# Two transformer blocks on one core: the order of seven block products, and where their neighbours' tiles lie

## The chip, the core and the metric

The kernel runs on one core of a Trainium2 chip, in one launch. The metric is the device time in microseconds (us), as the median of several runs. TensorE (PE) multiplies, ScalarE (ACT) and VectorE (DVE) move results out of its accumulation banks and prepare its operands, GpSimd (POOL) and SyncE (SP) issue most of the transfers. All engines run side by side, each through its own queue in order.

## What is computed

1,024 tokens of width 1,024 go through two blocks. The first is attention, a residual layer norm, and a feed-forward part with a short convolution; the second is a gated linear attention and a squared-ReLU feed-forward part. The two feed-forward parts are what the change is about:

```python
def conv_ffn(x, w_up, conv_w, conv_b, w_down):          # first block, d_ff 2816
    u = x @ w_up
    u = sum(u_pad[:, j:j + s, :] * conv_w[j] for j in range(3)) + conv_b
    value, gate = jnp.split(u, 2, axis=-1)
    return (value * jax.nn.gelu(gate)) @ w_down
def sqrelu_mlp(h, w1, w2):                              # second block, d_ff 4096
    return jnp.square(jax.nn.relu(h @ w1)) @ w2
x = layer_norm(DEEPNORM_ALPHA * x + mix, ln1_g, ln1_b)  # ahead of conv_ffn
h_lat = h_lat + mod_l[2] * o_lat                        # ahead of sqrelu_mlp
```

All is float32. The kernel makes each product of three passes: both operands are split into a high part (a rounded copy) and a low part (the rest), and high·high, high·low and low·high are summed.

## The kernel before

The stages run one after the other. Attention takes the first 500 us of the profile. `mixed` (L1006) then multiplies by `w_out`, normalizes and leads into the first **up pass** (609 to 1083 us); `ffn_down` (L1071) is the first **down pass**, with the context half of the second block woven in (1085 to 1405); the gated attention follows (to 1790); `o_projection` (L1267) multiplies by `w_o`, adds the residual and leads into the second up pass (1928 to 2279); `mlp_down` (L1314) is the second down pass and the end (from 2291).

**The up pass** (`up_pass`, L704) works on pairs of 128 weight columns, 22 pairs in the first block and 16 in the second. A pair is a 2x2 block product done with seven block multiplications in place of eight (Winograd's form). On the right stand seven fixed operands made from the activations, four in `hi`/`lo`, three in the extra tile `E` (`operands`, L675, writes them one token tile at a time). On the left stand A11, A12, A22 (the weights, loaded as `a` and `b`), and sums of them S1 to S4 (`sums`, L713). `parts` (L699) splits each into high and low; those tiles come from a ring of four slots (`ring`, L730), three of which a pair uses, and a smaller tile for S4. The loads and sums of a pair run more than one pair ahead of its products.

One `product` (L736) is twelve matmuls of 512 columns. The seven go into three accumulation banks X, Y and Z of eight. X is used for four partial sums in turn: after each product ACT copies X out, and the next product adds onto it, which it may do only when that copy has been read. The result is gathered in `ga` and `gb` in SBUF. The lines of the loop (L764 to L778), with their products in the order of the program:

```python
X  = A11·B11   -> ACT.copy(ga[xs], X)                       # L765, L766
Z  = A12·B21   -> DVE: ga[xs] = Z + ga[xs]                  # L767, L768
X += S2·T2     -> ACT.copy(ga[ys], X)                       # L769, L770
Y  = S1·T1                                                  # L771
X += S3·T3     -> ACT.copy(gb[ys], X)                       # L772, L773
                  DVE: gb[ys] = Y + gb[ys]                  # L774
Y += S4·B22    -> DVE: ga[ys] = Y + ga[ys]                  # L775, L776
X += A22·T4    -> ACT.copy(gb[xs], X)                       # L777, L778
```

TensorE keeps this order (`issue_after`, L739). The first pair is done in two halves of 256 columns, since the last token tiles come late. `finish` then runs on `ga` and `gb`: `conv_gate` (L1050) in the first block, with two ACT passes at L1055, four DVE passes at L1056 and L1057, a GELU, a product, and a store to HBM; `relu2` (L1301) in the second. In the first block `ga` and `gb` are the same two tiles for every pair; in the second they alternate.

**Ahead of the up pass** `square_product` (L622) makes each token tile in two halves of 512 columns, and `done` adds the residual, normalizes the row (a square with a sum on ACT, an inverse root on POOL), transposes (`rows`, L650) and calls `operands`. In `o_projection` the residual comes half a row at a time into the one buffer of pool `xp` (L1280, L1281). While the last tiles go through this, `up_pass` already loads and splits the first pair's A11, A12 and S2 (L719 to L722).

**The down pass** (`down_group`, L782) works on groups of hidden chunks (four in the second block). Each chunk is loaded back from HBM (`gload`, L789) and split, its weights likewise (`wdraw`, L795), and 16 units (8 token tiles by 2 halves) accumulate over the group and are added to `res`. Its pools (L1075, L1317) are laid on the bytes that the up pass has left, from the lowest address up, in the order in which they are opened; with `reuse_waits="tile"` a tile waits for the old tiles on its own bytes alone. Instructions are laid out by a scheduler that works through a modelled timeline when the kernel is built: what it puts first in an engine's queue comes first.

Of the kernel before, what the change touches and what calls it, by code (L numbers as in the profile page):

```python
# [17 lines left out]
P = 128  # L18
D = 1024
# [35 lines left out]
def build(tc, I, out, dbg=None, stop=None):  # L55
# [83 lines left out]
    convc = const.tile([P, 2 * NCH, 4], F32, name="convc")  # L139
# [48 lines left out]
    def attention_phase():  # L188
# [106 lines left out]
        for t, n in ((cs, "cs"), (convc, "conv"), (ng, "norms"), (adab, "ada_b_p"), (ghead, "ghead")):  # L295
            SP.dma_start(out=t, in_=I[n])
# [353 lines left out]
    def rows(src, t, scale=None, shift=None, by_row=None):  # L650

        if by_row is not None:
            diag = small.tile([P, P], F32, tag="diag", name="diag", bufs=2)
            DVE.tensor_scalar(out=diag, in0=ident, scalar1=by_row, scalar2=None, op0=ALU.mult)
# [20 lines left out]
    def operands(t, E, sp):  # L675
# [8 lines left out]
        split(by_k(u), E[0][:, 8:12, toks(t)], E[1][:, 8:12, toks(t)])  # L684
        DVE.tensor_tensor(out=b1[:, YS], in0=b1[:, YS], in1=u, op=ALU.subtract)
        DVE.tensor_tensor(out=b2[:, XS], in0=b2[:, YS], in1=b2[:, XS], op=ALU.subtract)
        split(by_k(b1), E[0][:, 0:8, toks(t)], E[1][:, 0:8, toks(t)])
        split(by_k(b2), hi[:, :, toks(t + 4)], lo[:, :, toks(t + 4)])

    def open_ext(st, n):  # L690
        pl = pool(st, n, 1, side="right")
        return [pl.tile([P, 12, 512], F32R, name=f"{n}_{x}") for x in ("hi", "lo")]

    def right_operands(E):

        at = {"B11": (0, 0, 0), "B21": (0, 4, 0), "T3": (0, 0, 512), "B22": (0, 4, 512), "T1": (1, 0, 0), "T4": (1, 4, 0), "T2": (1, 8, 0)}
        return {n: [tuple(a[:, k0 + k, c0:c0 + 512] for a in ((hi, lo), E)[e]) for k in range(4)] for n, (e, k0, c0) in at.items()}
# [6 lines left out]
    def up_pass(W, pairs, E, w0, room, finish):  # L704
# [16 lines left out]
        A1 = parts(a, w0)  # L721
        S20 = parts(ga[:, YS], w0, 512, "s")  # L722
# [7 lines left out]
        def ring():  # L730
            rot.rotate(-1)
            return rot[0]

        B = right_operands(E)
# [10 lines left out]
        for n in range(pairs):  # L745
            if n == 0:
                a, b, ga, gb = first
                A11, A12 = A1
                (S2,) = S20
                (S1,) = parts(ga[:, XS], w2, 512, "q")  # L750
                (S4,) = parts(gb[:, XS], w2, 512, "q")
                S3, A22 = parts(b, ring())
            else:
# [3 lines left out]
                A11, A12 = parts(a, ring())  # L757
                S1, S2 = parts(s, ring())
                (S4,) = parts(u, w2, 512, "q")
                S3, A22 = parts(b, ring())  # L760
# [696 lines left out]
```

## Time and profile before

| | |
|---|---|
| median of 3 runs | 2659.89 us (2654.38 to 2660.42) |
| the profiled execution | 2664.75 us, span 2663.0 us, mean granted TensorE clock 0.982 |
| TensorE, VectorE, ScalarE, GpSimd busy | 2498.9, 1640.1, 1154.2, 384.6 us |
| TensorE busy in the first, second up pass (609 to 1085, 1930 to 2279) | 435.4 of 476, 314.9 of 349 us |
| TensorE busy in the second down pass (2291 to 2606) | 312.5 of 315 us |

Busy time of TensorE counts each matmul to its modelled end, so matmuls overlap in it, and 100% is not the peak. The span leaves out 1.75 us of the profiled execution. Waits are named by what ended them.

### The profile page before, as it was taken

To read this page: it belongs to the slowest core of one execution; us is meant where nothing else is said; L and a number is where in the kernel's file an instruction comes from. 1 tells how busy PE (TensorE), PEld (TensorE's weight loads), DVE (VectorE), ACT (ScalarE), POOL (GpSimd) and SP (SyncE) were. 2 spreads that over 40 slices of the span, in tenths; PEclk is the share of its full clock that TensorE was granted. 3 is DMA by queue.
4 is the path that set the end of the run, shared out by engine and by line. 5 is a ranking of instruction groups with operands and counts; after the bars stand their busy time and mean duration, and the time that the engine had idled before them with its cause. 6 is when DMAs were issued, how large, how long until landed. Compare 5 with 4: busy or idle time off the path is not lost. (4 is left out here: it accounts for less than half of the span.)

```text
span 2663.0 us, 36063 instructions
## 1 busy us (share of the span) xinstructions
PE 2498.9 (94%) x13146; PEld 2117.1 (79%) x13146; DVE 1640.1 (62%) x3069; ACT 1154.2 (43%) x2046; POOL 384.6 (14%) x591
## 2 busy tenths in 40 slices
PE   8999999997999999899999999999879999899997
PEld 8898888776777777688888988997767777688885
DVE  5767675677776676587568666535754443355574
ACT  5555565544444444633236444323444444421212
POOL 4675623310000000000021000001100000000000
PEclk9999999998999999999999999999989999899998
DMA  5333322332222211645311211213322222543332
GB/s 169 109 87 103 91 73 83 120 124 95 74 77 79 79 72 48 208 148 184 110 72 59 74 52 60 74 36 128 107 95 96 102 95 86 173 144 101 121 107 91
DMA packets 130609, 266.81 MB, mean 100 GB/s; under 512 B 16376, under 2 KB 48760, under 8 KB 130432
## 3 DMA queue, kind: packets, MB, share of 16 engines
q1 hardware_dynamic: 120224, 227.81, 26.8%
q0 software_dynamic: 10208, 36.71, 3.4%
q8 instruction: 103, 1.69, 0.3%
q14 instruction: 74, 0.61, 0.1%
HBM read 205.17 MB, written 50.89 MB: 96 GB/s over the span
## 5 line engine op out<-in xcount | busy, mean ns | idle before, releaser
L130 PE MATMUL down<-wdh,gh 128*128 128x512 f32 x864 | 336.6, 397 | 24.1 <-ACT gh L102 12.3
L131 PE MATMUL down<-wdl,gh 128*128 128x512 f32 x864 | 338.3, 393 | 0.6 <-DVE wdl L103 0.6
L132 PE MATMUL down<-wdh,gl 128*128 128x512 f32 x864 | 333.8, 392 | 0.1
L130 PE MATMUL s<-act_hi,uh 128*128 128x512 f32 (+1 forms) x640 | 251.2, 393 | 67.9 <-DVE res L774 56.3
L132 PE MATMUL s<-act_hi,ul 128*128 128x512 f32 (+1 forms) x640 | 246.6, 385 | 3.0 <-DVE ul L103 3.0
L131 PE MATMUL s<-act_lo,uh 128*128 128x512 f32 (+1 forms) x640 | 246.4, 385 | 0.0
L130 PEld LDWEIGHTS down<-wdh,gh 128*128 128x128 f32 x864 | 163.6, 190 | 62.2 <-ACT gh L102 13.1
L130 PEld LDWEIGHTS s<-act_hi,uh 128*128 128x128 f32 x640 | 123.0, 192 | 107.4 <-DVE res L774 72.8
L569 POOL TENSOR_TENSOR rstd<-rstd,mhalf 128x1 f32<-128x1 f32 x74 | 55.2, 748 | 1012.3 <-DVE rstd L568 571.7
L131 PEld LDWEIGHTS down<-wdl,gh 128*128 128x128 f32 x864 | 164.0, 190 | 34.5 <-DVE wdl L103 1.3
L132 PEld LDWEIGHTS down<-wdh,gl 128*128 128x128 f32 x864 | 162.8, 189 | 35.2 <-DVE gl L103 1.1
L103 DVE TENSOR_TENSOR ul<-res,uh 128x1024 fp32r<-128x1024 f32 (+1 forms) x82 | 97.1, 1184 | 147.9 <-ACT uh L102 147.9
L130 PE MATMUL s<-ext_hi,uh 128*128 128x512 f32 (+1 forms) x480 | 183.2, 382 | 2.9 <-ACT res L766 2.9
L131 PE MATMUL s<-ext_lo,uh 128*128 128x512 f32 (+1 forms) x480 | 183.1, 382 | 0.0
L132 PE MATMUL s<-ext_hi,ul 128*128 128x512 f32 (+1 forms) x480 | 183.1, 381 | 0.0
L102 ACT CAST wdh<-wdraw 128x512 fp32r<-128x512 f32 x108 | 66.8, 622 | 194.0 <-PE down L132 71.0
L130 PE MATMUL tokp<-wh,act_hi 128*128 128x256 f32 (+1 forms) x512 | 147.3, 290 | 1.5 <-ACT wh L102 1.5
L132 PE MATMUL tokp<-wh,act_lo 128*128 128x256 f32 (+1 forms) x512 | 146.7, 288 | 1.9 <-DVE act_lo L103 1.9
L131 PE MATMUL tokp<-wl,act_hi 128*128 128x256 f32 (+1 forms) x512 | 147.5, 289 | 0.0
L132 PEld LDWEIGHTS s<-act_hi,ul 128*128 128x128 f32 x640 | 123.2, 192 | 27.1 <-DVE ul L103 3.3
L131 PEld LDWEIGHTS s<-act_lo,uh 128*128 128x128 f32 x640 | 123.3, 193 | 22.4
L369 ACT ACTIVATE P<-P,mx 128x640 f32<-128x640 f32 (+7 forms) x128 | 94.4, 738 | 77.6 <-DVE mx L366 73.6
(325 smaller groups left out, 6303.7 us busy)
## 6 DMA issues: line engine op xcount, KB each, us to landing
ada_w<-in_ada_w SPq DMA_DIRECT2D x192, 128.0 KB, 2.2
res<-in_w_up SPq DMA_DIRECT2D x44, 512.0 KB, 3.5
res<-in_mlp_w SPq DMA_DIRECT2D x32, 512.0 KB, 3.5
g2d<-res POOLq DMA_DIRECT2D x32, 512.0 KB, 2.9
wdraw<-in_mlp_w SPq DMA_DIRECT2D x64, 256.0 KB, 2.9
gload<-g2d SPq DMA_DIRECT2D x32, 512.0 KB, 3.5
g1d<-res POOLq DMA_DIRECT2D x22, 512.0 KB, 2.9
wdraw<-in_w_down SPq DMA_DIRECT2D x44, 256.0 KB, 3.3
```

What stands on the lines that cost most here:

```text
L102: ACT.copy(h, raw)
L103: DVE.tensor_tensor(out=l, in0=raw, in1=h, op=ALU.subtract)
L130: PE.matmul(out=o, lhsT=ah, rhs=bh, start=first, stop=False, **kw)
L131: PE.matmul(out=o, lhsT=ah, rhs=bl, start=False, stop=False, **kw)
L132: return PE.matmul(out=o, lhsT=al, rhs=bh, start=False, stop=last, **kw)
L369: ACT.activation(Pm[:, 0:W], Pm[:, 0:W], AF.Exp, bias=mx[:, 0:1], scale=-1.0, accum_out=mx[:, 1:2])
L569: POOL.tensor_tensor(out=t[:, 1:2], in0=t[:, 0:1], in1=mhalf, op=ALU.pow)
```

## The change

1. **Order of the products.** In `up_pass` Y = S1·T1 goes to second place and is copied at once into `gb[xs]` by ACT, S2·T2 follows, then Z. The addition that used to read Y at L774 now adds two SBUF tiles, after the product S4·B22. There is one ACT copy more in a pair, and the parts of `b` are split ahead of those of S4.
2. **First pair.** S1 and S2 are both split ahead of the pass, in pool `w0`; S3, A22 and S4 of the first pair get a high priority. The ring's four slots are laid anew.
3. **Down pools.** A function `down_pools` lays weights, raw loads, the rest and the chunk tiles in that order; the second down pass has eight weight slots for six, and groups of 2, six times 4, 3 and 3 chunks in place of eight times 4.
4. **Residual rows.** In `o_projection` the residual is loaded as whole rows straight into `res[t]`, after the last weight load of that batch, with no buffer between; pools there wait by tile.
5. **Small things.** The convolution weights are loaded at the start of the up pass, not at the start of the kernel; the squares of the row norms are written into `E` and not into a tile of their own; the diagonal tile of `rows` and `E` move to other pools or are cut in two tiles.

```diff
-    def up_pass(W, pairs, E, w0, room, finish):
+    def up_pass(W, pairs, E, w0, room, finish, setup=None):
...
         sums(a, b, ga, gb[:, XS])
-        A1 = parts(a, w0)
-        S20 = parts(ga[:, YS], w0, 512, "s")
+        A1, S12 = parts(a, w0), parts(ga, w0, tag="s")
         yield
...
-        w1, sw, w2 = (pool(st, n, b, reuse_waits="tile") for n, b in (("uw1", 1), ("usw", 2), ("uw2", 2)))
-        rot = deque((w0, w1, w2, w2))
+        sw, w2 = (pool(st, n, 2, reuse_waits="tile") for n in ("usw", "uw2"))
+        rot = deque(((w0, "s"), (w2, "w"), (w2, "w"), (w0, "w")))
...
-                (S2,) = S20
-                (S1,) = parts(ga[:, XS], w2, 512, "q")
-                (S4,) = parts(gb[:, XS], w2, 512, "q")
-                S3, A22 = parts(b, ring())
+                S1, S2 = S12
+                with tc.high_priority():
+                    S3, A22 = ring(b)
+                    (S4,) = parts(gb[:, XS], w2, 512, "q")
...
-                X, Z, Y = acc("s", m), acc("s", m), acc("s", m)
+                X, Y, Z = acc("s", m), acc("s", m), acc("s", m)
                 product(X, A11, "B11", True, cols)
                 ACT.copy(ga[:, xs], X)
+                product(Y, S1, "T1", True, cols)
+                ACT.copy(gb[:, xs], Y)
+                product(X, S2, "T2", False, cols)
+                ACT.copy(ga[:, ys], X)
                 product(Z, A12, "B21", True, cols)
                 DVE.tensor_tensor(out=ga[:, xs], in0=Z, in1=ga[:, xs], op=ALU.add)
-                product(X, S2, "T2", False, cols)
-                ACT.copy(ga[:, ys], X)
-                product(Y, S1, "T1", True, cols)
                 product(X, S3, "T3", False, cols)
                 ACT.copy(gb[:, ys], X)
-                DVE.tensor_tensor(out=gb[:, ys], in0=Y, in1=gb[:, ys], op=ALU.add)
                 product(Y, S4, "B22", False, cols)
                 DVE.tensor_tensor(out=ga[:, ys], in0=Y, in1=ga[:, ys], op=ALU.add)
+                DVE.tensor_tensor(out=gb[:, ys], in0=gb[:, xs], in1=gb[:, ys], op=ALU.add)
                 product(X, A22, "T4", False, cols)
                 ACT.copy(gb[:, xs], X)
...
+    def down_pools(st, n, w, mid, g):
...
+        wa = [pl(f"wd{i}", 2) for i in range(2)]
+        wdr, gr = pl("wdr", 2), pl("gr", 2)
+        wa.append(pl("wd2", w - 4))
...
+        mids = [pl(*m) for m in mid]
+        return (wdr, gr, in_turn("gp", g), wdp), mids
...
         def done(t, half, psum, last):
             c = slice(half * 512, half * 512 + 512)
             r = res[t]
-            x = xp.tile([P, 512], F32, tag="x", name="x2res")
-            SP.dma_start(out=x, in_=x2d[t][:, c])
-            DVE.tensor_tensor(out=r[:, c], in0=psum, in1=x, op=ALU.add)
+            if t not in seen:
+                with tc.issue_after(last.ins):
+                    SP.dma_start(out=r, in_=x2d[t])
+            DVE.tensor_tensor(out=r[:, c], in0=psum, in1=r[:, c], op=ALU.add)
...
-        groups = [list(range(i, i + 4)) for i in range(0, NMLP, 4)]
+        groups = [[0, 1]] + [list(range(i, i + 4)) for i in range(2, NMLP - 6, 4)] + [list(range(i, i + 3)) for i in (NMLP - 6, NMLP - 3)]
```

## Rows read from the trace of the kernel before

**Rows 1.** The page: busy time of TensorE, and the granted clock in 40 slices of the span.
```profile
PE 2498.9 (94%) x13146; PEld 2117.1 (79%) x13146; DVE 1640.1 (62%) x3069; ACT 1154.2 (43%) x2046; POOL 384.6 (14%) x591
...
PEclk9999999998999999999999999999989999899998
```

**Rows 2.** Groups of instructions over the whole span: line, engine, operation, tiles, count, then busy us, mean ns of one, and idle time of the engine ahead of them with what ended it.
```profile
L130 PE MATMUL s<-act_hi,uh 128*128 128x512 f32 (+1 forms) x640 | 251.2, 393 | 67.9 <-DVE res L774 56.3 <-ACT uh L102 6.7 <-ACT res L770 4.5
```

**Rows 3.** The chain that ended last, in order of time (start us, us, what), over one pair of the second up pass.
```profile
2000.03 0.59 ACT res L773
2000.65 0.70 DVE res L774
2001.39 0.51 PE s L130
...
2021.57 0.70 DVE res L774
```

**Rows 4.** Timeline of TensorE in the up passes: start us, duration us, the matmul, and in brackets the idle time ahead of it. First two matmuls without a wait, 56 steps apart, then the first and the last of the 36 waits of this kind.
```profile
1060.57 0.39 PE L131 MATMUL s<-ext_lo,uh 128*128 128x512 f32 x1
...
1073.39 0.39 PE L130 MATMUL s<-act_hi,uh 128*128 128x512 f32 x1
...
659.37 0.50 PE L130 MATMUL s<-act_hi,uh 128*128 128x512 f32 x1 [1.40 <-DVE res L774]
...
2273.39 0.51 PE L130 MATMUL s<-act_hi,uh 128*128 128x512 f32 x1 [1.40 <-DVE res L774]
```

**Rows 5.** Busy time by stretch: from:to, length, then busy us and count of PE, weight loads, DVE, ACT, POOL, then the granted clock, the share of the DMA engines and GB/s.
```profile
590.00:643.00 53.00, 38.33 (x232) 34.79 (x231) 42.33 (x66) 25.24 (x40) 5.76 (x8) 0.84 0.25 90
699.00:720.00 21.00, 19.60 (x86) 15.78 (x85) 14.75 (x17) 9.46 (x11) 0.53 (x1) 1.00 0.21 75
1083.00:1112.00 29.00, 21.21 (x89) 15.75 (x88) 22.69 (x31) 25.14 (x42) 3.27 (x4) 0.94 0.96 339
1910.00:1965.00 55.00, 35.83 (x231) 33.68 (x232) 37.01 (x66) 24.64 (x45) 4.29 (x7) 0.78 0.25 80
2000.00:2021.00 21.00, 19.53 (x84) 15.70 (x84) 8.85 (x11) 9.96 (x13) 1.06 (x2) 1.00 0.27 101
2279.00:2296.00 17.00, 5.45 (x14) 4.16 (x14) 4.44 (x8) 6.39 (x7) 1.06 (x2) 0.60 0.87 292
2560.00:2606.00 46.00, 43.47 (x192) 35.65 (x192) 35.20 (x54) 8.34 (x13) 0.00 (x0) 1.00 0.44 143
```

**Rows 6.** Timeline of VectorE in one pair of the first up pass.
```profile
953.70 0.69 DVE L714 TENSOR_TENSOR s<-res 128x512 f32<-128x512 f32 x1 [1.55 <-DMA res<-in_w_up]
...
956.24 0.68 DVE L776 TENSOR_TENSOR res<-s,res 128x512 f32<-128x512 f32 x1
...
959.44 1.22 DVE L103 TENSOR_TENSOR ul<-res,uh 128x1024 fp32r<-128x1024 f32 x1
960.57 1.28 DVE L1057 SCALAR_TENSOR_TENSOR res<-res,convc,res 128x1022 f32<-128x1022 f32 x1
```

**Rows 7.** Timeline of ScalarE in the same pair.
```profile
956.96 1.25 ACT L1055 ACTIVATE res<-res,convc 128x1024 f32<-128x1024 f32 x1 [1.29 <-DVE res L776]
...
961.94 0.59 ACT L766 COPY res<-s 128x512 f32<-128x512 f32 x1 [1.04 <-DVE res L1057]
...
968.78 1.05 ACT L102 CAST uh<-res 128x1024 fp32r<-128x1024 f32 x1 [1.93 <-PE s L131]
```

**Rows 8.** Timeline of TensorE in the first pair of each up pass: matmuls with a wait ahead of them.
```profile
622.70 0.39 PE L130 MATMUL s<-act_hi,uh 128*128 128x256 f32 x1 [4.54 <-ACT res L770]
...
1939.99 0.58 PE L130 MATMUL s<-act_hi,uh 128*128 128x256 f32 x1 [6.75 <-ACT uh L102]
...
1948.52 0.58 PE L130 MATMUL s<-act_hi,uh 128*128 128x256 f32 x1 [2.24 <-DVE res L774]
```

**Rows 9.** Timeline of VectorE at the end of `o_projection`: the last two additions of the residual.
```profile
1915.27 0.69 DVE L1282 TENSOR_TENSOR res<-sq,x2res 128x512 f32<-128x512 f32 x1 [1.62 <-DMA x2res<-x2d]
...
1919.20 0.69 DVE L1282 TENSOR_TENSOR res<-sq,x2res 128x512 f32<-128x512 f32 x1 [1.71 <-DMA x2res<-x2d]
```

**Rows 10.** Timeline of TensorE at the start of the two down passes and of the last group: matmuls with a wait.
```profile
1085.62 0.95 PE L130 MATMUL down<-wdh,gh 128*128 128x512 f32 x3 [2.14 <-ACT wdh L102]
...
1095.74 0.50 PE L130 MATMUL down<-wdh,gh 128*128 128x512 f32 x1 [3.15 <-ACT res L1088]
...
2290.74 0.80 PE L130 MATMUL down<-wdh,gh 128*128 128x512 f32 x1 [11.55 <-ACT gh L102]
...
2605.13 0.74 PE L130 MATMUL down<-wdh,gh 128*128 128x512 f32 x2 [2.53 <-ACT wdh L102]
```

**Rows 11.** Timeline of SyncE's queue at the end of the second up pass.
```profile
2279.62 0.42 SPq L618 DMA_DIRECT2D fg<-in_final_g  x1
2280.09 0.95 SPq L789 DMA_DIRECT2D gload<-g2d  x2
```

**Rows 12.** The view of the `res` tiles in the first up pass: time from a DMA's issue to its landing, of the weight loads.
```profile
DMA to landing us min/median/max: 2.9/3.4/4.4
```

**Rows 13.** The same line in the view of the tile `gload`: all loads of hidden chunks in the down passes.
```profile
DMA to landing us min/median/max: 3.1/3.8/10.6
```

**Rows 14.** Groups of instructions over the whole span: the additions of the second down pass.
```profile
L1333 DVE TENSOR_TENSOR res<-res,down 128x512 f32<-128x512 f32 x112 | 75.4, 684 | 85.0 <-PE down L132 84.7
```

More of the change, by code (lines that the diff above doesn't have):

```diff
@@ L138, in build @@
     cs = const.tile([P, 16], F32, name="cs")
-    convc = const.tile([P, 2 * NCH, 4], F32, name="convc")
     m2d = tc.dram_tile([P, D], F32, name="m2d")
@@ L648, in by_k, with rows @@
         return a.rearrange("p (k t) -> p k t", t=P)
-    def rows(src, t, scale=None, shift=None, by_row=None):
+    def rows(src, t, scale=None, shift=None, by_row=None, pl=None):
         if by_row is not None:
-            diag = small.tile([P, P], F32, tag="diag", name="diag", bufs=2)
+            diag = pl.tile([P, P], F32, tag="diag", name="diag", bufs=2)
             DVE.tensor_scalar(out=diag, in0=ident, scalar1=by_row, scalar2=None, op0=ALU.mult)
@@ L780, in up_pass, with pl, in_turn, get @@
         st.close()
+    def down_pools(st, n, w, mid, g):
+        def pl(name, bufs):
+            return pool(st, f"{name}{n}", bufs, reuse_waits="tile")
+        def in_turn(name, counts):
+            rot = deque(p for i, b in enumerate(counts) for p in [pl(f"{name}{i}", b)] * b)
+            def get():
+                rot.rotate(-1)
+                return rot[-1]
+            return get
+        wa = [pl(f"wd{i}", 2) for i in range(2)]
+        wdr, gr = pl("wdr", 2), pl("gr", 2)
+        wa.append(pl("wd2", w - 4))
+        rot = deque(p for p, b in zip(wa, (2, 2, w - 4)) for _ in range(b))
+        def wdp():
+            rot.rotate(-1)
+            return rot[-1]
+        mids = [pl(*m) for m in mid]
+        return (wdr, gr, in_turn("gp", g), wdp), mids
     def down_group(chs, gd, W, pools, evac, tile_outer=False, by_col=None):
@@ L789, in chunk @@
             SP.dma_start(out=r, in_=gd[ch])
-            g[ch] = gp.tile([P, T], F32R, tag="gh", name="gh"), gp.tile([P, T], F32R, tag="gl", name="gl")
+            pl = gp()
+            g[ch] = pl.tile([P, T], F32R, tag="gh", name="gh"), pl.tile([P, T], F32R, tag="gl", name="gl")
             split(r, *g[ch])
@@ L1010, in mixed @@
         g, b = aux.tile([P, D], F32, name="ln1g"), aux.tile([P, D], F32, name="ln1b")
-        junk = aux.tile([P, D], BF16, name="junk")
         mv = {}
@@ L1048, in build, with conv_weights @@
     g1d = [tc.dram_tile([P, T], F32, name=f"g1d{c}") for c in range(NCH)]
+    convc = []
+    def conv_weights(st):
+        convc.append(pool(st, "convc", 1, reuse_waits="tile").tile([P, 2 * NCH, 4], F32, name="convc"))
+        SP.dma_start(out=convc[0], in_=I["conv"])
     def conv_gate(n, gv_, gg_):
@@ L1126, in ffn_down @@
         hi, lo = (actp.tile([P, KD, T], F32R, name=n) for n in ("act2_hi", "act2_lo"))
-        gb.extend(gp.tile([P, D], F32, tag=c, name=f"ln2{c}") for c in ("gh", "gl"))
+        pl = gp()
+        gb.extend(pl.tile([P, D], F32, tag=c, name=f"ln2{c}") for c in ("gh", "gl"))
         bcast(gb[0], "ln2_g")
@@ L1271, in o_projection @@
             transposed(res[t], t)
-        aux, sp, xp, wo = pool(st, "aux", 1), pool(st, "sp", 1), pool(st, "xp", 1), pool(st, "wo", 8)
-        m, junk = aux.tile([P, D], F32, name="m2b"), aux.tile([P, D], BF16, name="junk")
+        aux, sp, wo = (pool(st, n, b, reuse_waits="tile") for n, b in (("aux", 1), ("sp", 1), ("wo", 8)))
+        m = aux.tile([P, D], F32, name="m2b")
         SP.dma_start(out=m, in_=m2d)
```

46 lines of the change are left out of this document (24 added, 22 removed).

## Prediction

> **What bounds the kernel now.** I read the page first. TensorE is busy 94% of the span and its granted clock is near full in nearly all slices [rows 1]. Busy time counts overlapping matmuls to their modelled ends, so 94% does not say how often TensorE stood still. The view for that is its idle time by group: the matmuls that open a product on `act_hi` waited 67.9 us in all, 56.3 of it for DVE's L774 [rows 2]. The chain in order of time shows how: ACT copies X (0.59), DVE adds Y to that copy (0.70), and only then TensorE goes on [rows 3]. TensorE writes S4·B22 onto bank Y, which L774 has still to read; L774 needs the copy of S3·T3, the product just ahead. So two steps of two engines stand between two neighbouring products. The timeline of TensorE shows the wait as 1.40 us of idle time, the same in the first and the last of 36 pairs [rows 4].
>
> The other idle time lies at joints, where the views by stretch show TensorE well below its length: the start of both up passes, the change to both down passes, and the last group [rows 5]. There the clock falls too: 0.84, 0.94, 0.78 and 0.60 of full as means, so part of those stretches ran at 1.2 GHz, while a steady pair, with its 1.40 us of idle time, stays at 1.00 [rows 5].
>
> **The steady pairs.** A pair takes 2021.57 − 2000.65 = 20.92 us [rows 3]. Undisturbed matmuls follow each other in (1073.39 − 1060.57) / 56 = 0.229 us [rows 4], so the 84 matmuls of a pair need 19.23. The difference, 1.69 us, is the idle time with the refill behind it. In the new order each bank has a whole product (12 × 0.229 = 2.75 us) between a product and the next write onto the same bank: Y stands between the first two of X, Z between the next, S4·B22 ahead of the last, and Y's copy has three products' time. An ACT copy is 0.59 [rows 7], so all is covered if ACT is free within 2.1 us. The addition of L774 is no longer one that TensorE waits for; its cost stays on DVE, and one ACT copy (0.59) is added. Per pair of the first pass DVE then has 14.75 us and ACT 9.46 + 0.59 = 10.1, of 19.23 [rows 5]; neither becomes the bound as a sum. Gain: 36 × 1.69 = **60.8 us**, bounds 25 (rival A) and 61.
>
> **What is late next.** In the first pass `ga` is one buffer. X's copy at L766 waited until DVE had done L1057 of the pair before [rows 7]; it ends at 962.5, and TensorE needed it about 0.9 us later, two products into the pair. That chain (L776, L1055, the convolution, L766) starts at the product S4·B22 in the old and the new order, with the same three products ahead of it. So it holds with 0.9 us to spare, plus or minus what the scheduler puts between. What stood in it were the sums of a later pair, which waited 1.55 us for a weight load [rows 6]. That load is issued when the parts of `b` are split. Its slot is freed by S1·T1 and S2·T2; in the old order by the fourth product, in the new by the third. So the load goes out up to 2.75 us earlier, which about makes up for the 1.69 that the pair gets shorter. Rival A is the case in which it doesn't.
>
> **First pairs.** From 590 to 643 us TensorE is busy 38.3 of 53 [rows 5], with 4.54 in one wait behind ACT [rows 8]. S1 ready ahead, and T1, T2 of the first tokens written early, let three products run before the last tiles are done; but DVE is busy 42.3 of those 53 us with the norms, and the second half of the pair waits for that. I take 7 back, bounds 0 and 11. In the second block, from 1910 to 1965, it is 35.8 of 55 at a clock of 0.78 [rows 5]. Two things go. The last residual additions come 3.9 us apart, each waiting for a load into the one buffer [rows 9], and end about 9.5 us after the last product; with whole rows loaded before, they follow the product. And the waits of 6.75, 2.24 and about 3 between are for splits that now come ahead [rows 8]. 9.5 + 12 would be 21; part of it is again DVE's work on the last tiles. I take 18, bounds 5 and 25. The whole-row loads stand in SP's queue behind the batch's last weight load; even a landing of 10.6, the longest of such a size [rows 13], is two products of 24 × 0.229 and there are four banks: nothing.
>
> **Up to down.** At 2290.74 TensorE had waited 11.55 [rows 10]. SP issued the chunk loads only at 2280.09, behind a load of `final_g` at 2279.62 [rows 11], both after the pass had ended: their bytes were those of the last pair. The new order of pools puts the first weights on tiles freed one pair earlier and the raw loads on the raw sums, also free; `final_g` moves beyond them. What remains is X's last copy, behind two ACT passes, some 1 to 2 us. With the lower clock (0.60 over 17 us [rows 5]) I take 12, bounds 6 and 14. In the first block the joint cost 2.14 + 3.15 [rows 10] plus smaller ones, in a stretch whose DMA engines are 0.96 busy [rows 5], and the evacuation still waits for the last convolution: 4, bounds 0 and 8.
>
> **Second down pass.** Nine groups for eight: 16 more additions of 0.684 on DVE [rows 14], beside matmuls. The group before the last now takes 16 × 9 × 0.229 = 33 us for 44, and has the same 32 additions (22 us); DVE was busy 35.2 in 46 us there [rows 5], so 13 went to operands, for four chunks; three need 10. 22 + 10 of 33 is tight, so the wait of 2.53 at the start of the last group [rows 10] may grow. I take +3, bounds −4 and +8. The tail behind the last matmul does not change. The moved convolution load, the diagonal and the square's target cost nothing that I can find: off every chain named above.
>
> **Sum.** −60.8 − 7 − 18 − 12 − 4 + 3 = −98.8, and 2664.75 − 98.8 = 2566. The median of before lies 4.9 below the profiled execution; I go half of that and say **2564**. Its own range, from the bounds of the joints: 2542 to 2586.
>
> **Rivals.** **A, the convolution's chain takes the wait over.** If ACT's queue has the parts of S1, S2 (freed by the fourth product now) ahead of those of `b`, the way from the end of that product is two casts (1.05 each [rows 7]), one `ul` (1.22 [rows 6]), a landing of 3.4 [rows 12], four sums (2.6), L776, L1055, two passes of 1.28, one `ul`, L766: 15.5 us for the five products until X is needed, 13.75. That is 1.7 per pair in 21 pairs, 36 us: 2600. For it: the old queue had exactly this wait in it. Against: the scheduler takes what is ready, and `b` is ready first.
>
> **B, the joints give nothing back** (the loads come early but ACT or DVE run them late, or in front of what TensorE needs): 60.8 − 3, so 2605.
>
> **C, the wait has another cause.** The Trainium skill, Perfetto Trace Analysis, section Optimization Strategy, says that one gap repeating on the engine that should be saturated can mean too little SBUF or PSUM for the next tile. By that rule a new order of products would leave the gap where it is. As a mechanism here: a pair takes three of eight banks, and a product would wait for a bank or a slot. The rows name L774, a reader of the bank itself [rows 4], so it has little for it. It would give 2664.75 − 38 = 2627, some 2625 for the median.
>
> **D, slower.** The same loop as A, with a longer landing: earlier loads of the down passes and whole rows don't reach into the steady pairs, but if weight loads did land in 10.6 [rows 13] instead of 3.4 [rows 12], the loop would cost 1.7 + 7.2 = 8.9 in 21 pairs, 187 us: 2664.75 − 98.8 + 187, about 2750. It ends slower than before from a landing of 6.4 on (98.8 / 21 = 4.7, less 1.7, on top of 3.4). Against it: DMA engines 0.21 to 0.27 busy there [rows 5], and 4.4 as the longest landing [rows 12]. The Trainium skill, DMA: Bandwidth & Descriptors, section Issuing engines are not separate DMA queues, speaks for it: all issuers share the same 16 engines and interleave, so a load moved forward takes its share from those beside it. The trace shows such a crowd only at the joints (0.96, 0.87 [rows 5]).
>
> **How the numbers follow.** Forecast 0.66; A 0.13; B 0.10; C 0.04; D 0.03; a gain above the bounds 0.04. The range reaches from the forecast's lower end to A: 2542 to 2602, leaving out B's outer part, C and D. A difference of 0.3% (8 us) is what can be told from none. Faster by more: all but D and a little of C and B combined, 0.95; within 0.3%: 0.02; slower: 0.03.
>
> **What would show it.** Right: no waits of TensorE for L774; steady pairs 19.2 to 19.4 us apart in both passes at clock 1.00; the first chunk load issued ahead of the last pair's end and under 3 us between the passes; DVE's last residual additions a product apart. Wrong: a wait per pair behind ACT's L766 with L1057 or a weight load ahead of it (A, D); TensorE idle over 5 us at 1930 to 1950 or between the passes (B); the same 1.4 us with another name (C). The forecast falls if both passes still lose a microsecond in each pair.

## The result, and the profile after

The changed kernel takes 2566.57 us (median of 4 runs, 2565.24 to 2569.72) against 2657.14 for the kernel before beside it (2653.83 to 2660.42): a ratio of 0.966, with a 95% interval of 0.964 to 0.968. The forecast was 2564, the range 2542 to 2602. The profiled execution took 2567.65, with a span of 2565.9 against 2663.0 before. In medians the change is worth 90.6 us; the two profiled executions lie 97.1 apart, since the one of before took 2664.75, 7.6 above the median beside it, and the one of after 1.1 above its own.

The page of the changed kernel, its lines for TensorE's busy time and the granted clock, and the group of matmuls that open a product [rows 1, 2]:

```profile
PE 2476.6 (97%) x13146; PEld 2119.5 (83%) x13146; DVE 1649.8 (64%) x3079; ACT 1172.1 (46%) x2084; POOL 384.8 (15%) x591
...
PEclk9999999998999999899999999999989999999999
...
L130 PE MATMUL s<-act_hi,uh 128*128 128x512 f32 (+1 forms) x640 | 244.2, 382 | 1.0 <-ACT res L772 1.0
```

The idle time of 67.9 us ahead of those matmuls is 1.0, and the adding line is no longer named. The timeline of TensorE shows where it went and what is new (start, duration, matmul, idle time ahead of it):

```profile
36.22 0.77 PE L360 MATMUL S<-Y,X 128*128 128x128 f32 x2 [2.40 <-DMA Y<-Z]
...
646.98 0.50 PE L130 MATMUL s<-ext_4hi,uh 128*128 128x512 f32 x1 [0.70 <-ACT res L768]
...
1053.82 1.12 PE L91 MATMUL ctp<-ident,ctx_x 128*128 128x128 f32 x4 [7.47 <-ACT ctx_x L973]
...
1059.91 1.11 PE L91 MATMUL ctp<-ident,ctx_x 128*128 128x128 f32 x4 [4.97 <-ACT ctx_f L606]
...
1061.99 0.80 PE L130 MATMUL down<-wdh,gh 128*128 128x512 f32 x1 [0.43 <-ACT gh L102]
...
2000.48 0.39 PE L130 MATMUL s<-ext_4hi,uh 128*128 128x512 f32 x1
...
2019.52 0.39 PE L130 MATMUL s<-ext_4hi,uh 128*128 128x512 f32 x1
...
2204.78 0.50 PE L130 MATMUL down<-wdh,gh 128*128 128x512 f32 x1 [2.18 <-ACT gh L102]
```

The rows at 2000.48 and 2019.52 are the last L130 of S2·T2 in two neighbouring pairs: 84 matmuls in 19.04 us, no wait among them [rows 4 had 1.40 in each pair]. The second down pass now waits 2.18 where it waited 11.55 [rows 10]. But the first one starts 16 us after the last product, behind two transposes of the context that stand ahead of it in TensorE's queue, and its own last wait, 0.43, is for ScalarE's split of the first chunk. The attention phase has a wait of 2.40 at 36 us. The stretches that answer to [rows 5]:

```profile
699.00:720.00 21.00, 21.00 (x94) 17.38 (x94) 15.98 (x19) 10.15 (x13) 0.53 (x1) 1.00 0.21 76
1046.00:1075.00 29.00, 16.13 (x68) 13.26 (x67) 20.79 (x31) 22.99 (x40) 3.13 (x5) 0.71 0.93 332
1873.00:1917.00 44.00, 33.74 (x237) 32.64 (x236) 38.16 (x73) 27.02 (x49) 4.84 (x8) 0.84 0.33 108
2000.00:2021.00 21.00, 21.00 (x94) 17.39 (x93) 8.76 (x11) 11.25 (x14) 1.07 (x2) 1.00 0.33 112
2202.00:2212.00 10.00, 7.82 (x35) 6.16 (x34) 3.56 (x4) 7.25 (x10) 1.07 (x2) 1.00 0.91 293
```

TensorE fills these two steady stretches whole. The start of the second up pass has about as many matmuls in 11 us less, with DVE busy 38 of 44; the start of the first down pass is the one stretch of these that is worse (16.1 of 29 at 0.71, against 21.2 of 29 at 0.94). The second down pass now starts at a granted clock of 1.00, where it was 0.60.

Where the time went, by stage. Each value is worked out from the starts of the first and the last matmul of the stage in the timeline (`sq`, `s` and `down` name them); "first pair" reaches from the last `sq` to the first matmul of the second pair, "pairs" from there to the last `s`, and a "joint" from the last `s` to the first `down`.

| stage, us | before | after | order alone | old order | 64 bytes |
|---|---|---|---|---|---|
| attention, to the first `sq` | 502.1 | 507.5 | 502.1 | 508.3 | 501.8 |
| square product 1 | 94.2 | 91.0 | 93.3 | 91.0 | 90.5 |
| first pair 1 | 46.1 | 42.1 | 42.1 | 48.0 | 47.7 |
| 21 pairs | 440.7 | 405.3 | 405.7 | 437.6 | 436.9 |
| joint 1 | 2.5 | 16.0 | 2.6 | 17.3 | 2.5 |
| down pass 1 | 309.0 | 300.0 | 310.3 | 299.4 | 306.5 |
| linear attention | 407.1 | 405.5 | 406.1 | 405.9 | 401.8 |
| square product 2 | 107.5 | 106.0 | 108.3 | 106.8 | 108.0 |
| first pair 2 | 56.0 | 43.4 | 49.8 | 47.7 | 55.7 |
| 15 pairs | 313.6 | 285.4 | 288.2 | 310.8 | 310.8 |
| joint 2 | 12.0 | 2.6 | 10.5 | 2.1 | 11.7 |
| down pass 2 | 356.8 | 350.0 | 356.6 | 350.0 | 356.6 |
| behind the last matmul | 15.6 | 11.2 | 15.5 | 11.2 | 15.5 |
| span | 2663.0 | 2565.9 | 2591.1 | 2636.1 | 2646.0 |

Each column is one execution. Stages whose code is the same differ by 2 to 5 us between these kernels (linear attention 401.8 to 407.1), so a single difference of that size in this table shows nothing by itself.

### The profile page after: what moved, and what is told of

Its sections match the earlier page's. It is cut to its first block, busy times and chain, and to the rows that moved or that the text cites. A ratio compares the mean times of both kernels' runs of the same rounds, so it can differ in the third digit from the quotient of the medians.

```text
span 2565.9 us, 36138 instructions
## 1 busy us (share of the span) xinstructions
PE 2476.6 (97%) x13146; PEld 2119.5 (83%) x13146; DVE 1649.8 (64%) x3079; ACT 1172.1 (46%) x2084; POOL 384.8 (15%) x591
## 4 chain that ended last, share of the span: by engine, by line
PE 82%; DVE 8%; DMA 4%; ACT 3%; issue 2%; POOL 1%; SPq 0%; DVEq 0%; POOLq 0%; ACTq 0%
PE s L130 8%; PE s L131 8%; PE s L132 8%; PE down L130 7%; PE down L131 7%; PE down L132 7%; PE proj L130 3%; PE proj L132 3%; PE proj L131 3%; PE tokp L130 3%; PE tokp L132 3%; PE tokp L131 3%; PE y L414 2%; PE ptp L91 2%; PE sq L130 1%
## 5 line engine op out<-in xcount | busy, mean ns | idle before, releaser
L130 PE MATMUL down<-wdh,gh 128*128 128x512 f32 x864 | 341.1, 395 | 5.0 <-ACT gh L102 3.2
L130 PE MATMUL s<-act_hi,uh 128*128 128x512 f32 (+1 forms) x640 | 244.2, 382 | 1.0 <-ACT res L772 1.0
L130 PEld LDWEIGHTS down<-wdh,gh 128*128 128x128 f32 x864 | 162.7, 188 | 42.0 <-DVE res L1125 4.8
L103 DVE TENSOR_TENSOR ul<-res,uh 128x1024 fp32r<-128x1024 f32 x80 | 96.6, 1210 | 100.0 <-ACT uh L102 99.9
L130 PE MATMUL tokp<-wh,act_hi 128*128 128x256 f32 (+1 forms) x512 | 148.8, 293 | 0.9 <-ACT wh L102 0.9
L130 PEld LDWEIGHTS s<-act_hi,uh 128*128 128x128 f32 x640 | 122.0, 191 | 24.0 <-ACT res L772 1.5
L1369 DVE TENSOR_TENSOR res<-res,down 128x512 f32<-128x512 f32 x128 | 87.3, 684 | 80.0 <-PE down L132 80.0
L102 ACT CAST gh<-gload 128x1024 fp32r<-128x1024 f32 x54 | 57.0, 1057 | 162.5 <-PE down L131 126.8
L370 POOL TENSOR_SCALAR P<-P,mx 128x640 f32<-128x640 f32 (+7 forms) x128 | 95.8, 751 | 195.6 <-DVE mx L369 162.3
```

What stands on the lines that cost most here:

```text
L102: ACT.copy(h, raw)
L103: DVE.tensor_tensor(out=l, in0=raw, in1=h, op=ALU.subtract)
L130: PE.matmul(out=o, lhsT=ah, rhs=bh, start=first, stop=False, **kw)
L370: POOL.tensor_scalar(out=Pm[:, 0:W], in0=Pm[:, 0:W], scalar1=mx[:, 2:3], scalar2=0.0, op0=ALU.mult, op1=ALU.add)
L1369: DVE.tensor_tensor(out=r, in0=r, in1=psum, op=ALU.add)
```

## Experiments

The first two ask for the order of the products. **Order alone** is the kernel before with the new loop body and nothing else:

```diff
-                X, Z, Y = acc("s", m), acc("s", m), acc("s", m)
+                X, Y, Z = acc("s", m), acc("s", m), acc("s", m)
...
+                product(Y, S1, "T1", True, cols)
+                ACT.copy(gb[:, xs], Y)
+                product(X, S2, "T2", False, cols)
+                ACT.copy(ga[:, ys], X)
...
```

> The kernel before with the new order of the seven products and nothing else of the change. Theory W (the 1.40 us of idle time per pair is the two-step sum on bank Y): the waits behind L774 vanish, steady pairs fall from 20.92 to 19.0 to 19.5 us, 36 pairs give 50 to 68 us, so about 2590 to 2605 against 2657. Theory A (the convolution's chain takes the wait over, in the first pass alone): 2610 to 2630, with TensorE waiting for ACT's copy into ga. Theory C (too few banks or buffers): no change, 2650 or more. It also shows whether the spacing of undisturbed matmuls, 0.229 us before and 0.227 after, belongs to the order: if it does, a pair without waits takes 19.04; if it doesn't, 19.2 to 19.25.

Measured: 2592.76, ratio 0.977 (0.975 to 0.978). Two L130 of neighbouring pairs, each the last of S2·T2, in its timeline of TensorE:

```profile
2004.76 0.39 PE L130 MATMUL s<-ext_hi,uh 128*128 128x512 f32 x1
...
2023.99 0.39 PE L130 MATMUL s<-ext_hi,uh 128*128 128x512 f32 x1
```

A pair takes 19.23: the waits for L774 are gone, but matmuls still stand 0.229 apart. The pairs give 35.0 and 25.4 us (table), 60.4 in all. Theory W holds; A and C fall. The first pairs got shorter too, by 4.0 and 6.2. In that of the second block the waits for the sum are gone, those for splits are still there:

```profile
1900.79 0.58 PE L130 MATMUL s<-act_hi,uh 128*128 128x256 f32 x1 [5.21 <-ACT uh L102]
```

**Old order** is the other way round, the changed kernel with the old loop body.

> The changed kernel with the old order of the products; all else of the change stays. Theory W: the wait of about 1.4 us at the product S4 times B22 comes back in each pair, steady pairs 20.6 to 20.95 us, time 2615 to 2635 against 2566. Theory C, or a gain that came from the new pools and the cut operand tiles instead: 2566 to 2580.

Measured: 2640.03, ratio 0.995 (0.993 to 0.996), 5 us above what was expected. The wait is back, in the timeline of TensorE:

```profile
2018.77 0.50 PE L130 MATMUL s<-act_hi,uh 128*128 128x512 f32 x1 [1.40 <-DVE res L776]
...
2039.50 0.50 PE L130 MATMUL s<-act_hi,uh 128*128 128x512 f32 x1 [1.40 <-DVE res L776]
```

But the pair takes 20.73, not 20.92. The 0.19 is the spacing of the matmuls, 0.227 where it was 0.229, which came with something else in the change. The tiles' places are the candidate. In the built programs `act_hi` starts at 96 modulo 128 in both kernels; the parts of the weights (`uh`, `ul`) and the square product's weights start at 32 before and at 96 after, since a constant of 704 bytes and a diagonal of 1,024 left the space below them. **64 bytes** tests that on the kernel before:

```diff
     w0 = pool(w0_st, "w0", 1)
+    POOL.memset(w0.tile([P, 16], F32, tag="pad", name="pad"), 0.0)
...
     w0 = pool(w0_st, "w02", 1)
+    POOL.memset(w0.tile([P, 16], F32, tag="pad", name="pad"), 0.0)
```

> The kernel before with an unused tile of 64 bytes ahead of the first parts in each of the two up passes, and nothing of the change. Everything on top of it (parts of the weights, operands of the square products) moves by 64 bytes. Theory M (a matmul is 1% slower where the places of its two operands differ by 64 bytes modulo 128; in the built programs act_hi stands at 96 modulo 128 in both kernels, the parts and the square product's weights at 32 before and at 96 after): the spacing of s falls from 0.229 to 0.227, of sq from 0.233 to 0.227, steady pairs from 20.92 to 20.73, time 11 to 14 us less, 2641 to 2646 against 2656. Theory N (the spacing belongs to something else in the change): 2653 to 2659, pairs 20.92.

Measured: 2647.33 against 2655.64, ratio 0.997 (0.995 to 0.998); 8 us, somewhat less than expected. Its timeline of TensorE:

```profile
2008.01 0.50 PE L130 MATMUL s<-act_hi,uh 128*128 128x512 f32 x1 [1.40 <-DVE res L774]
...
2028.74 0.50 PE L130 MATMUL s<-act_hi,uh 128*128 128x512 f32 x1 [1.40 <-DVE res L774]
```

20.73, with the same wait: theory M holds here. An empty tile of 64 bytes is worth 3.8 and 2.8 us in the pairs and 3.7 in the first square product; the second one doesn't show it in its length (108.0 for 107.5), though its steps fell to 0.227 too.

**The attention phase.** In the changed kernel the queue of SyncE has four loads of `ada_w` in a stretch ahead of the first copy of Z into Y, and the last three stand there for 5.37 us:

```profile
24.20 0.33 SPq L150 DMA_DIRECT2D ada_w<-in_ada_w  x1
24.58 0.42 SPq L121 DMA_DIRECT2D raw<-in_wqk  x1
28.19 5.37 SPq L150 DMA_DIRECT2D ada_w<-in_ada_w  x3
33.65 1.16 SPq L222 DMA_DIRECT2D Y<-Z  x2
```

In the **conv dummy** the weights of the convolution are loaded at their old place too, into a tile that nothing reads:

```diff
+        convx = f1.tile([P, 2 * NCH, 4], F32, name="convx")
-        for t, n in ((cs, "cs"), (ng, "norms"), (adab, "ada_b_p"), (ghead, "ghead")):
+        for t, n in ((cs, "cs"), (convx, "conv"), (ng, "norms"), (adab, "ada_b_p"), (ghead, "ghead")):
```

> The changed kernel with a second, unused load of the convolution's weights at the place in the attention phase where the kernel before loaded them. Theory Q (without that load the scheduler put one more load of ada_w ahead of the first copies of Z into Y in SP's queue; they go out 1.4 us later, and TensorE waits 2.4 us for them and then runs at the lower clock for a while): the order of the queue is that of before again, the wait at 33.5 us vanishes, the attention phase ends 4 to 6 us earlier than in the changed kernel, 2560 to 2563. Theory R (the 5.4 us are a difference from run to run): attention as in the changed kernel, 2565 to 2569.

Measured: 2566.07, ratio 0.966 (0.965 to 0.968). The same part of its SyncE queue:

```profile
24.44 7.03 SPq L150 DMA_DIRECT2D ada_w<-in_ada_w  x3
31.53 1.16 SPq L222 DMA_DIRECT2D Y<-Z  x2
```

There are three, the copies go out 2.1 us earlier, the wait of 2.40 is gone, and the phase ends at 502.0. In the changed kernel and the seven variants of it without the extra load it ends between 505.3 and 508.3, in the two with it at 502.0 and 502.5. So theory Q holds for the phase. The time doesn't show the 3 to 6 us that were expected: the second square product, the same code, took 3.8 us longer in the profiled execution, and the median can't be told from the changed kernel's.

**Joint 1.** The convolution's weights moved into the up pass, where their tile lies under the second buffer of the chunk loads of the first down pass (104,160 and 103,136 to 107,232 in the built program). The queue of SyncE in the changed kernel, and the last reader of that tile on VectorE:

```profile
1027.34 16.42 SPq L824 DMA_DIRECT2D wdraw<-in_w_down  x2
...
1054.81 1.02 SPq L817 DMA_DIRECT2D gload<-g1d  x2
```

```profile
1052.62 1.28 DVE L1092 SCALAR_TENSOR_TENSOR res<-res,convc,res 128x1022 f32<-128x1022 f32 x1
```

In **conv low** the tile is opened ahead of the raw sums:

```diff
+        if setup:
+            setup(st)
         sw, w2 = (pool(st, n, 2, reuse_waits="tile") for n in ("usw", "uw2"))
...
-        if setup:
-            setup(st)
```

> The changed kernel with one allocation moved: the tile of the convolution's weights is opened ahead of the raw sums and parts of the up pass, not behind them, so that it no longer lies under the second buffer of the chunk loads of the first down pass. Theory U (those loads waited for the last convolution of the up pass, which reads that tile): the first chunk loads go out before or about when the up pass ends, the joint from the last product to the first of the down pass falls from 16 us to 3 to 6, time 2554 to 2558. Theory V (the context's transposes, queued ahead of the down pass, and its loads hold TensorE up, wherever the tile lies): the joint stays at 13 to 17 us, 2564 to 2569.

Measured: 2574.80, ratio 0.970 (0.968 to 0.971), slower than the changed kernel though the joint did what U says. SyncE's queue, then the timeline of TensorE:

```profile
1043.83 0.33 SPq L817 DMA_DIRECT2D gload<-g1d  x1
```

```profile
1050.23 1.65 PE L130 MATMUL down<-wdh,gh 128*128 128x512 f32 x3 [3.71 <-ACT wdh L102]
...
1054.14 0.79 PE L130 MATMUL down<-wdh,gh 128*128 128x512 f32 x1 [1.28 <-ACT wdh L102]
...
1061.63 0.66 PE L91 MATMUL ctp<-ident,ctx_x 128*128 128x128 f32 x4 [1.82 <-ACT ctx_x L973]
...
1063.64 0.79 PE L130 MATMUL down<-wdh,gh 128*128 128x512 f32 x1 [1.34 <-ACT res L1123]
```

The first chunk load goes out before the up pass ends (1046), 11 us earlier than in the changed kernel. The joint fell from 16.0 to 4.1, and the pass grew from 300.0 to 314.5: the one long wait became several shorter ones. (This profiled execution, 2580.42, is the slowest of its four, and some 9 us of it lie in linear attention and the second square product, which the edit doesn't touch.) The move of 704 bytes also put half of the parts at 32 modulo 128, and pairs took 19.12 to 19.17 where they had taken 19.04. **Joint late** takes 768 bytes instead, so that all remainders stay, and lets the context begin later:

```diff
-CTXSHARE = 60000
+CTXSHARE = 65000
+CTXLATE = 5000
...
+        yield CTXLATE
         gate_weights()
...
+        convc.append(pool(st, "convc", 1, reuse_waits="tile").tile([P, 2 * NCH + 4, 4], F32, name="convc"))
...
```

> The changed kernel with the tile of the convolution's weights under the raw sums, as in the run that moved it, but of 768 bytes, so that all places above keep their remainder modulo 128; and the context's work begins 5,000 units of its plan later, so that its loads and transposes stand behind the first products of the down pass. Theory X (in the run that moved the tile the joint got 12 us shorter and the pass 15 longer, since loads and splits of the context and of the first groups then collided; the context can wait): joint 3 to 5 us, the first down pass from joint to last product 300 to 306, time 2554 to 2560. Theory Y (the first 60 us of that pass are bound by what the DMA engines and ACT must do there in any order): joint plus pass 314 to 319 as before, time 2564 to 2569.

Measured: 2569.27, ratio 0.968 (0.967 to 0.970). Pairs are at 19.04 again, which is what the remainder modulo 128 says. Joint and pass are 4.1 and 310.9, together 315.0, the sum that theory Y gives. Its timeline of TensorE:

```profile
1045.91 0.96 PE L131 MATMUL down<-wdh,gh 128*128 128x512 f32 x3 [3.69 <-ACT wdh L103]
...
1058.88 0.80 PE L131 MATMUL down<-wdh,gh 128*128 128x512 f32 x1 [6.12 <-ACT res L1125]
```

The wait is now for ScalarE's copy of the first results out of their banks. That copy (at 1058.26) stands in ScalarE's queue behind a wait for the context's rows and, after it, a table load of 1.28 and casts of the context's weights:

```profile
1052.23 1.06 ACT L590 ACTIVATE ctx_f<-ctx_x 128x1024 f32<-128x1024 f32 x1 [1.71 <-DMA ctx_x<-in_ctx]
```

The window from 1044 to 1075:

```profile
1044.00:1075.00 31.00, 22.52 (x87) 17.54 (x88) 21.50 (x31) 24.21 (x41) 2.89 (x4) 0.83 0.90 324
```

ScalarE is busy 24 of 31 us and the DMA engines 0.90, much as in the changed kernel (23 of 29, 0.93). That these two are the bound in any order, as theory Y has it, isn't shown: the kernel before had them busier (25 of 29, 0.96 [rows 5]) and TensorE at 0.94 of its clock there, against 0.83 here. Nor did the edit put all of the context's work behind the first copies, so theory X was tried only in part.

**Old pools**: the second down pass on pools in the order of before.

```diff
-        pools, (rp, fc, ar, ac) = down_pools(st, 2, 8, (("rp", 2), ("fc", 1), ("ar", 2), ("ac", 1)), (3, 5))
+        wdp, wdr, gr, gp, rp, fc, ar, ac = (pool(...) for n, b in (("wdp2", 8), ("wdr2", 2), ("gr2", 2), ("gp2", 8), ...))
+        pools = wdr, gr, lambda: gp, lambda: wdp
```

> The changed kernel with the second down pass on pools in the order of before (weights, raw weights, raw chunks, chunks), sizes and groups as changed. Theory of the prediction (what the tiles lie on sets when the first loads may go): the joint of the second up pass to the second down pass grows from 2.6 to 9 to 12 us, the first chunk load goes out after the pass has ended, time 2573 to 2577. Rival (the shorter first group alone made the joint short): joint 2.5 to 5 us, 2565 to 2570.

Measured: 2570.24, ratio 0.968 (0.967 to 0.969). TensorE and SyncE at the joint:

```profile
2205.06 3.78 PE L130 MATMUL down<-wdh,gh 128*128 128x512 f32 x8 [6.74 <-ACT wdh L102]
```

```profile
2195.64 0.33 SPq L617 DMA_DIRECT2D fg<-in_final_g  x1
...
2197.50 0.36 SPq L817 DMA_DIRECT2D gload<-g2d  x1
```

The joint is 7.1, between the theories: 4.5 of the 9.4 us come from the order of the pools. What gave the other 4.9 isn't shown; it isn't the shorter first group, since the joint is 2.6 with groups of four too. In time the run can't be told from the changed kernel's second measurement (2570.26, below). The first chunk load goes out 0.4 us before the last matmul of the up pass (2197.9); in SyncE's queue of the changed kernel it went out 27 us ahead of that matmul (2202.2):

```profile
2175.21 0.42 SPq L817 DMA_DIRECT2D gload<-g2d  x1
```

**Groups of four** and **no preparation, six slots** ask where the second down pass became 11 us shorter.

```diff
-        groups = [[0, 1]] + [list(range(i, i + 4)) for i in range(2, NMLP - 6, 4)] + ...
+        groups = [list(range(i, i + 4)) for i in range(0, NMLP, 4)]
```

> The changed kernel with the second down pass in eight groups of four chunks again; its pools stay. Theory G (the groups of three at the end and the pair at the start shorten the pass, since fewer loads and splits stand ahead of the last group): first to last matmul of the pass 355 to 358 us instead of 350, a wait of some 2.5 us at the start of the last group, the way from the last matmul to the end 14 to 16 us instead of 11, time 2574 to 2580. Theory P (the 11 us came from the pools or from the places of the tiles): 2564 to 2569.

Measured: 2566.89, ratio 0.966 (0.965 to 0.968); the pass takes 350.0, with 10.2 behind it. Theory G falls: the groups are worth nothing that can be seen. The next edit goes further:

```diff
-        A1, S12 = parts(a, w0), parts(ga, w0, tag="s")
+        A1 = parts(a, w0)
...
-                S1, S2 = S12
-                with tc.high_priority():
+                S1, S2 = parts(ga, w0, tag="s")
...
-        pools, (rp, fc, ar, ac) = down_pools(st, 2, 8, ...
+        pools, (rp, fc, ar, ac) = down_pools(st, 2, 6, ...
```

(with the groups of four as well)

> The changed kernel with two parts undone that lie far from each other and are read by stage. One: in the first pair of each up pass S1 and S2 are split after the pass is opened, and the parts of b and S4 without priority. Theory of the prediction (splits made ahead shorten the first pairs): from the last square product to the first steady pair 3 to 6 us more in the first block (42 in the changed kernel), 4 to 10 in the second (43). Two: the second down pass in eight groups of four with six slots for its weights, as before, still on the new pools. Theory S (the eight slots took the last splits out of the last group; with six, two tiles of the last group can be split only 13 us before its end): from the first product of that pass to the end of the span 366 to 372 us instead of 361, with 14 to 16 us behind the last matmul. Rival (places or order of the pools gave it): 359 to 362. Time, by both theories, 2578 to 2588; by the rivals 2566 to 2570.

Measured: 2576.81, ratio 0.971 (0.970 to 0.972). The pass takes 356.7 with 15.6 behind it, as before. TensorE waits at the start of the last group again, as in [rows 10], and VectorE makes the last split of weights late:

```profile
2520.98 1.22 PE L130 MATMUL down<-wdh,gh 128*128 128x512 f32 x2 [2.56 <-ACT wdh L102]
```

```profile
2549.86 1.37 DVE L103 TENSOR_TENSOR wdl<-wdraw,wdh 128x512 fp32r<-128x512 f32 x2 [2.05 <-ACT wdh L102]
```

That split is 13 us ahead of the last matmul (2563.0). In the changed kernel the last one comes 31 us ahead of it:

```profile
2523.84 0.69 DVE L103 TENSOR_TENSOR wdl<-wdraw,wdh 128x512 fp32r<-128x512 f32 x1
```

What comes late bunches at the end: 12 of the 16 multiplications by `final_g` on VectorE (L1385) run behind the last matmul, where the changed kernel has 4. So eight slots for six account for most of the 11 us: the 4.4 behind the pass, and some 4 to 5 in its last group, waits and the matmuls at the lower clock after them. About 2 of the pass is something else: its first ten matmuls or so stand 0.427 us apart in this run and in the kernel before, at a granted clock of 0.62 and 0.53, so mostly at 1.2 GHz; in the changed kernel they stand 0.227 apart at 1.00.

The first pairs took 40.9 and 39.2, not longer than in the changed kernel (42.1, 43.4): preparing splits ahead is worth nothing that can be seen.

**Half rows**: the residual in halves through one buffer again.

```diff
+        xp = pool(st, "xp", 1, reuse_waits="tile")
...
-            if t not in seen:
-                with tc.issue_after(last.ins):
-                    SP.dma_start(out=r, in_=x2d[t])
-            DVE.tensor_tensor(out=r[:, c], in0=psum, in1=r[:, c], op=ALU.add)
+            x = xp.tile([P, 512], F32, tag="x", name="x2res")
+            SP.dma_start(out=x, in_=x2d[t][:, c])
+            DVE.tensor_tensor(out=r[:, c], in0=psum, in1=x, op=ALU.add)
...
```

> The changed kernel with the residual rows of the second block loaded in halves through one buffer again. Theory of the prediction (the last additions wait for those loads): the additions come 3.5 to 4 us apart at the end, the stretch from the last square product to the first steady pair grows by 5 to 10 us, time 2571 to 2577. Rival (the norm's own work sets that stretch, or the whole rows themselves make TensorE wait in the square products): 2562 to 2569.

Measured: 2573.40, ratio 0.969 (0.968 to 0.971). On VectorE the last additions are about 4 us apart again (4.5 between the last two), as in [rows 9]:

```profile
1876.99 0.69 DVE L1319 TENSOR_TENSOR res<-sq,x2res 128x512 f32<-128x512 f32 x1 [1.25 <-DMA x2res<-x2d]
...
1881.48 0.69 DVE L1319 TENSOR_TENSOR res<-sq,x2res 128x512 f32<-128x512 f32 x1 [0.94 <-DMA x2res<-x2d]
```

In the changed kernel four of them run as one row of 2.48:

```profile
1872.53 2.48 DVE L1319 TENSOR_TENSOR res<-sq,res 128x512 f32<-128x512 f32 x4 [2.60 <-PE sq L132]
```

So its additions end 1.6 us after the square product's last matmul has started, and here 11.9. Less than half of that comes through: the first pair took 47.2 for 43.4, 4 us, under the 5 to 10 that were expected. It is one execution of each; all variants with whole rows have 38.8 to 44.2.

**Best** puts joint late, the unused load and slots of 2,176 bytes for the attention's weights together, and **after again** is the changed kernel beside it.

```diff
+            w = 544 if m == 528 else m
-            h = wp.tile([P, m], F32R, tag="wh", name="wh")
+            h = wp.tile([P, w], F32R, tag="wh", name="wh")[:, 0:m]
...
```

> The run before this one with two more edits: the unused load of the convolution's weights in the attention phase, which restores the order of SP's queue there, and slots of 2176 bytes, not 2112, for the weights of the attention phase, so that all of them stand at 96 modulo 128, like act_hi. Theory M: the projections' matmuls that take 0.231 us fall to 0.227, 2 to 5 us over the attention phase; with the queue's order the phase ends at 497 to 500 us instead of 507. Time 5 to 9 us under the run before this one.

> The changed kernel itself, beside the others on the same chip: 2564 to 2569, to compare them within a few us.

Measured: 2567.86 (0.967, 0.966 to 0.969) and 2570.26 (0.968, 0.967 to 0.970). In **best** the attention phase ends at 502.5, not at 497 to 500, and 0.5 later than with the unused load alone: the aligned slots gave the projections nothing, and their matmuls stayed at a median of 0.232. The intervals overlap, so no version is shown to beat the changed kernel.

## Why the prediction was right, and where it was not

**Steady pairs, −60.8.** The order alone gives −60.4. In the changed kernel it is 35.4 + 28.2 = 63.6. The matmuls also stand 0.227 us apart there instead of 0.229 [rows 4], which shows in the second pass (28.2 for 25.4) and hardly in the first (35.4 for 35.0): its 21 pairs lose 5.4 us in stops, half of it in stops too short for the view below, against 2.1 with the order alone. What is late next was named rightly, X's copy into `ga` (L768): the view of TensorE's waits between 641 and 1046 us has it.

```profile
PE s L130 <- ACT res L768: 1.7, 5, 0.7
PE s L130 <- ACT res L772: 1.0, 1, 1.0
```

The 0.9 us to spare were nearly enough: 1.7 us in all 21 pairs together where rival A had 36. C falls, since the gap went with nothing changed but the order. D's condition isn't there: weight loads land in a median of 3.5 us.

**First pairs, −7 and −18.** Measured −7.2 and −14.1, each with its square product. The reason was partly wrong, and that −7 met −7.2 is luck: the first pair itself gave 4.0. The step that failed is that S1 ready ahead lets three products run: without the preparation nothing was lost. The order itself gave 4.0 and 6.2. The waits in [rows 8] hint at it: 4.54 names X's copy, and 2.24, put down to a split, names the sum L774. The two that are for splits (6.75 and about 3) stay with the order alone, 5.21 and 2.65, and are gone in the changed kernel, but also in the run that splits S1 and S2 late; which part of the change took them away isn't shown. The rest is the 64 bytes in the first block (3.7) and, on one execution's evidence, whole rows in the second (4); another 4 there has no cause that was tried, and is no more than the scatter of such stages.

**Up to down, second block, −12.** Measured −9.4, and 2.3 more in the next pass, whose first matmuls no longer stand 0.427 apart; the forecast had counted the clock in. The mechanism is as told as far as the order of the pools goes (4.5): first chunk load early, 2.18 us of wait left for ScalarE's split. The rest has no cause shown.

**Up to down, first block, −4.** Here the sign was wrong: joint and pass together took 316.0 for 311.5. Two steps failed. The moved convolution load was costed at nothing for its transfer alone; its tile blocked a chunk load until the last convolution was done. And the joint was costed as if a wait removed there were gained: with the joint at 4 us the pass gave it all back. So the tile explains the long joint and not the longer sum. What makes joint and pass together 4 us longer than with the old pools is open; the kernels with old pools there have 309 to 313, those with the new ones 315 to 319. The work of ScalarE and the DMA engines in the first 30 us, and the lower clock there (0.71 to 0.83 against 0.94), are candidates that no run separates.

**Second down pass, +3.** Measured −6.8 in the pass and −4.4 behind it. The step counted additions and operands but not the slots. With six, TensorE waited at the start of the last group, its last two tiles could only be split 13 us before the end, and the last additions and final multiplications bunched behind that; "the tail does not change" fell for the same reason. Some 2 of the 6.8 are the clock at the start of the pass, told above.

**Not foreseen: +5.4 in the attention phase.** A load taken out there changed the order that the scheduler gave SyncE's queue. "Off every chain named above" was true of the load and not of its place in the queue.

So −97.1 in the span met −98.8 partly by chance: −14 in the second down pass stands against +8.5 at joint 1, +5.4 in attention and 4 less in the second block's first pair. That the absolute 2564 was met leans on a second accident: the sum started from an execution 7.6 us above the later median, and 2 of them were taken off; in medians the gain was 90.6. And the 2586 of the forecast's own range isn't what its terms' bounds add up to: −60.8 − 5 − 6 + 8 from 2664.75 is 2601.

## What to carry to other kernels

Where an accumulation bank waits for a reader that itself waits for another copy, reorder the products so that a whole product lies between a bank's last write and its next one; the gain could be read off pair length and matmul spacing beforehand, within 1% here (60.8 and 60.4). A wait removed at a joint may come back as several in the next stage, as it did here: measure joint and stage together. When a tile moves, look up what lies over and under its bytes, and give each group of weight tiles as many slots as its last user holds at once.

## What the runs showed of the hardware

Matmuls of 128x128 by 128x512 with both operands in SBUF stood 0.227 us apart where both tiles had the same remainder modulo 128 bytes, and 0.229 (up pass) or 0.233 (square products) where the remainders differed by 64; the figures are medians of the steps between neighbouring starts in the timeline, and the places are those in the built programs. Three shifts agree: 64 bytes on the kernel before (pairs 20.92 to 20.73), 704 bytes in conv low (19.04 to 19.12 and 19.17), 768 in joint late (19.04 again). `down` stood at 0.227 in both kernels, with both operands at 32 before and at 96 after. The projections of the attention phase don't follow it: at 0.232 they stayed with aligned tiles, so something else holds them, and why the remainder matters elsewhere isn't shown.
